# A hybrid encoder layer on one core: the first loads on two queues, the second input tile in halves

## The chip, the core and the metric

The kernel runs on one core of one Trainium2 chip. A core has a matrix engine (TensorE, in the profile PE, with its weight loads as PEld), a vector engine (VectorE, DVE), a scalar engine (ScalarE, ACT), GpSimd (POOL) and SyncE (SP). Each engine takes its instructions in order. A DMA is issued by an instruction on an engine's queue, SP's or ACT's here, and its bytes are moved by 16 DMA engines. A tile in the on-chip memory has 128 partitions. The metric is the time of one execution on the device in microseconds (us), the median of several runs.

## The reference, cut

The layer norms its input, projects it once into the columns of two attention mixers (a sliding window with grouped queries and sinks, and a neighbourhood attention on a grid of tokens), norms both results, projects them back, and ends with a gated MLP with a short convolution and a last norm. Sequence and width are both 1024.

```python
hn = rmsnorm(h, norm_mix[l])
proj = jnp.einsum('bsd,de->bse', hn, w_in[l])
qa, ka, va, qb, kb, vb = jnp.split(proj, splits, axis=-1)
...
o_a = window_gqa_sink(qa, ka, va, sink[l])
o_b = neighbourhood_attention(..., rpb[l])
mix = jnp.concatenate([rmsnorm(o_a, norm_a[l]), rmsnorm(o_b, norm_b[l])], axis=-1)
h = h + jnp.einsum('bse,ed->bsd', mix, w_out[l])
hn = rmsnorm(h, norm_ffn[l])
h = h + conv_gated_mlp(hn, w_gate[l], w_up[l], conv_w[l], conv_b[l], w_down[l])
return rmsnorm(h, norm_final)
```

The change lies at the start of the combined projection.

## The kernel before, in words

The input is held transposed, as eight tiles `xT[k]` of 128 features by 1024 tokens (k = 0 to 7, 512 KB each, 4 KB in a partition). The weights `w_in[m]` of one block of 128 output columns are 128 by 8 by 128; index j of the middle dimension belongs to input tile k = j.

Every product is made from two halves of precision: a float32 tile is split into a high part, rounded by ACT (a Copy into float32r), and a low part, the difference, made by DVE. So an input tile gives `xgh` and `xgl` (L125 and L126, and for the first tile L532 and L533), and a weight tile gives `whi` and `wlo` (L108 and L109, and for the first weights L537 and L538). One block of a product is three matmuls of 128x512: high by high (L113), the weights' high part by the input's low part (L114), the weights' low part by the input's high part (L115). The norm's gain is put in with the split, from a column of the parameters tile `par`; the factor 1/rms comes later, on the products.

The kernel starts with small memsets on GpSimd, a table load and a one-column activation (`warm`, L95) on ACT, and eight matmuls on `ones` (L98). Then the first two column blocks (`first`, m = 0 and 1) are projected together while the input arrives: for every input tile k, for each half h of the tokens, one block of three matmuls for m = 0 (into bank `pj`) and one for m = 1 (into bank `o`), so 12 matmuls for each tile (L566 to L571). For the squares that the norm needs, ACT squares each input tile (L139) and DVE adds them up (L141). The third block (m = 2, bank `s`) follows, then the sums for 1/rms (L150 to L161), and then the rest of the projections and the attention.

All loads of the head stand in SP's queue in this order: `par` (L82, 60 KB), the first half of input tile 0 (L522), the weights j = 0 of both blocks (L524, 64 KB each), the second half of tile 0 (L525), the weights j = 1 to 3 of both blocks (L527, 192 KB each), input tiles 1 to 3 whole (L515), the weights j = 4 to 7 of both blocks (L105), tiles 4 to 7 (L515), and then constants and further weights. The `raw` weights have two staging buffers and the high and low parts three each, so the loads of L105 wait until DVE has made the low parts of the first weights, and their split waits until PE has used the first weights; what stands behind such a load in SP's queue waits with it.

PE's instructions keep the order in which the code writes them (`manual_schedule`). The order of ACT, DVE, POOL and SP is made when the kernel is built, by a list scheduler that estimates when operands are ready and prefers what was written first.

Of the kernel before, what the change touches and what calls it, by code (L numbers as in the profile page):

```python
# [13 lines left out]
F32 = mybir.dt.float32  # L14
F32R = mybir.dt.float32r
AF = mybir.ActivationFunctionType
ALU = mybir.AluOpType
PSUM = bass.MemoryType.PSUM

D, S, HD = 1024, 1024, 64  # L20
KT = D // 128
NB = S // 128
HALF = 512
# [22 lines left out]
C_NMIX, C_NFFN, C_NFIN, C_NA, C_NB, C_CW, C_CB, C_SINK = 0, 8, 16, 24, 28, 32, 98, 120  # L46
# [5 lines left out]
def hybrid_layer(tc, xT, w_in, w_out, w_gate, w_up, w_down, small, sink, rpb, consts, rope, out):  # L52
    nc = tc.nc
    with ExitStack() as ctx:
# [6 lines left out]
        wpool = inner("weights", 3)  # L61
# [6 lines left out]
        def big(name, tag, dt=F32):  # L68
            return lpool.tile([128, S], dt, name=name, tag=tag, bufs=slots[tag])
# [7 lines left out]
        f32 = lambda ap: ap.bitcast(F32)  # L77
        tsl = lambda h: slice(h * HALF, (h + 1) * HALF)
        col = lambda c: par[:, c:c + 1]

        par = cpool.tile([128, C_END], F32, name="par")
        nc.sync.dma_start(par[:, 0:C_SINK], small)  # L82
        ones = cpool.tile([128, 128], F32, name="ones")
        nc.gpsimd.memset(ones, 1.0 / D)
        eps = cpool.tile([128, 1], F32, name="eps")
        nc.gpsimd.memset(eps, EPS)
        cst = cpool.tile([128, K_END], F32, name="cst")
        ident = cst[:, K_ID:K_ID + 128]


        ctx.enter_context(tc.manual_schedule(engines={mybir.EngineType.PE}))
# [20 lines left out]
        def block(ps, w, x, h, first, last):  # L112
            nc.tensor.matmul(ps, w[0], x[0][:, tsl(h)], start=first, stop=False)  # L113
            nc.tensor.matmul(ps, w[0], x[1][:, tsl(h)], start=False, stop=False)  # L114
            nc.tensor.matmul(ps, w[1], x[0][:, tsl(h)], start=False, stop=last)  # L115
# [7 lines left out]
        def split_scaled(src, scale, name, tag):  # L123
            hi, lo = big(name + "h", tag, F32R), big(name + "l", tag, F32R)
            nc.scalar.activation(hi, src, AF.Copy, scale=scale)  # L125
            nc.vector.scalar_tensor_tensor(lo, src, scale, f32(hi[:, :]), op0=ALU.mult, op1=ALU.subtract)  # L126
            return hi, lo
# [380 lines left out]


        xg, first = [None] * KT, [Project(0), Project(1)]  # L510
        xts, sqs = [], []

        def load_x(k):
            xt = big("xt", "op")
            nc.sync.dma_start(xt, xT[k])  # L515
            xts.append(xt)


        xt0 = big("xt", "op")
        xts.append(xt0)  # L520
        head = [[wpool.tile([128, 4, 128], dt, name="w0", tag=tag, bufs=n) for dt, tag, n in ((F32, "raw", 2), (F32R, "whi", 3), (F32R, "wlo", 3))] for _ in first]
        nc.sync.dma_start(xt0[:, 0:HALF], xT[0, :, 0:HALF])  # L522
        for p, (raw, _, _) in zip(first, head):
            nc.sync.dma_start(raw[:, 0:1], w_in[p.m, :, 0:1, :])  # L524
        nc.sync.dma_start(xt0[:, HALF:S], xT[0, :, HALF:S])  # L525
        for p, (raw, _, _) in zip(first, head):
            nc.sync.dma_start(raw[:, 1:4], w_in[p.m, :, 1:4, :])  # L527
        xg[0] = big("xgh", "xg", F32R), big("xgl", "xg", F32R)
        g0 = col(C_NMIX)

        def first_x(h):
            nc.scalar.activation(xg[0][0][:, tsl(h)], xt0[:, tsl(h)], AF.Copy, scale=g0)  # L532
            nc.vector.scalar_tensor_tensor(xg[0][1][:, tsl(h)], xt0[:, tsl(h)], g0, f32(xg[0][0][:, tsl(h)]), op0=ALU.mult, op1=ALU.subtract)  # L533

        def first_w(ks):
            for raw, hi, lo in head:
                nc.scalar.activation(hi[:, ks], raw[:, ks], AF.Copy)  # L537
                nc.vector.tensor_tensor(lo[:, ks], raw[:, ks], f32(hi[:, ks]), op=ALU.subtract)  # L538

        first_x(0)  # L540
        first_w(slice(0, 1))
        first_x(1)
        first_w(slice(1, 4))
        for p, (_, hi, lo) in zip(first, head):
            p.w = [(hi[:, j, :], lo[:, j, :]) for j in range(4)]
        for k in range(1, 4):
            load_x(k)
        for p in first:
            p.w += load_w(w_in[p.m, :, 4:8, :])
        for k in range(4, KT):  # L550
            load_x(k)
        nc.sync.dma_start(cst, consts)
        nc.sync.dma_start(par[:, C_SINK:C_END], sink.partition_broadcast(128))
        nsink = cpool.tile([128, 8], F32, name="nsink")
# [5 lines left out]
        for _ in range(2):  # L560
            t = quarters(big("f", "mix"))
# [2 lines left out]
        banks = [[bank("pj", "pj") for _ in range(2)], [bank("o", "o") for _ in range(2)]]  # L564
        acc = None
        for k in range(KT):  # L566
            if k:
                xg[k] = split_scaled(xts[k], col(C_NMIX + k), "xg", "xg")
            for h in range(2):
                for p, ps in zip(first, banks):  # L570
                    block(ps[h], p.w[k], xg[k], h, k == 0, k == KT - 1)  # L571
# [3 lines left out]
        raw, hi, lo = big("raw3", "mix"), big("whi3", "mix", F32R), big("wlo3", "mix", F32R)  # L575
# [84 lines left out]
        for g in range(2):  # L660
            for b in range(NB):
                q, t = unit_window(g, b)
# [49 lines left out]
        for u in range(len(flat)):  # L712
            q, t, need, kind = flat[u]
# [46 lines left out]
        for h in range(2):  # L760
            wide = widen(vb2[h], "pt")
            for i in range(4):
                x = mix[4 + i][:, tsl(h)]
                hi, lo = (t[:, tsl(h)] for t in mg[4 + i])
# [462 lines left out]
        for i, (p, j, c) in enumerate(order):  # L1227
            prepare(i + 6, i + 4)
            f, n = PARTS[c]
# [123 lines left out]
```

## Time and profile before

| What | Value |
|---|---|
| Median of 3 runs | 1135.11 us (1134.78 to 1135.58) |
| The profiled execution, its own time | 1135.27 us |
| Span that the profile covers | 1133.5 us |
| Mean granted TensorE clock | 0.983 |
| DMA traffic of the whole kernel | 147.03 MB, mean 130 GB/s |

The span is shorter than the execution's time by 1.8 us, which lie around the profiled instructions. A timeline row gives the start in us from the span's start, the length, the engine, the line of the kernel, the operation, the tile written and the tiles read, the shapes and a count; in brackets stands how long the engine had been idle before it, and what ended that idle time. In a view by stretches, a row gives for each engine the busy time in the stretch (and the number of instructions), then the clock granted to TensorE as a share of full speed, the mean busy share of the DMA engines and the GB/s that they moved. Starts of matmuls are taken from the trace; their ends are modelled, and matmuls overlap, so the distance between two starts is the pace.

### The profile page before, as it was taken

The numbers are of one execution on the slowest core, as the hardware profiler recorded it, in microseconds if no ns is written. First come the engines' busy times: TensorE is split into PE (matmuls) and PEld (weight loads), VectorE is DVE, ScalarE is ACT, GpSimd is POOL, SyncE is SP. The second block draws the span as 40 slices with busy tenths as digits, with TensorE's granted clock in tenths as the row PEclk, the third lists the DMA queues.
The fourth block names the chain that finished last, engine by engine and source line by source line (L and its number), as shares of the span: only waits on it lengthen the run. The fifth ranks groups of instructions, "written<-read, shape, count | busy, mean of one in ns | idle before, by whom it ended". The sixth has DMA issues, their size and how long they took to land.

```text
span 1133.5 us, 14918 instructions
## 1 busy us (share of the span) xinstructions
PE 1087.3 (96%) x5124; PEld 904.3 (80%) x5124; DVE 853.2 (75%) x1549; ACT 549.9 (49%) x1033; POOL 105.9 (9%) x186
## 2 busy tenths in 40 slices
PE   8969999999999989999899999999999899999995
PEld 6857888888878878888688888888888688888884
DVE  5556888766689667899988778877877868886843
ACT  6335777656667534444443344334343645543531
POOL 0302333232223100000000000000000000000001
PEclk8989999999999999999899999999999999999997
DMA  7252120333215217303432223222322698865723
GB/s 262 61 126 79 52 57 29 80 93 88 74 36 150 94 47 256 134 29 109 181 128 103 102 93 121 103 102 93 121 103 93 222 322 280 280 226 169 258 83 148
DMA packets 67708, 147.03 MB, mean 130 GB/s; under 512 B 8112, under 2 KB 16816, under 8 KB 67632
## 3 DMA queue, kind: packets, MB, share of 16 engines
q1 hardware_dynamic: 57552, 121.04, 33.4%
q10 hardware_dynamic: 10080, 25.04, 5.9%
q8 instruction: 40, 0.66, 0.2%
q14 instruction: 36, 0.29, 0.1%
HBM read 103.58 MB, written 28.57 MB: 117 GB/s over the span
## 4 chain that ended last, share of the span: by engine, by line
PE 87%; DVE 6%; DMA 2%; ACT 2%; issue 1%; SPq 0%; POOLq 0%; ACTq 0%; DVEq 0%
PE pj L113 7%; PE pj L114 7%; PE pj L115 7%; PE dn L797 6%; PE dn L799 6%; PE dn L798 6%; PE z L797 4%; PE z L798 4%; PE z L799 4%; PE s L273 3%; PE x L797 3%; PE x L798 3%; PE x L799 3%; PE y L799 3%; PE y L798 3%; PE y L797 3%
## 5 line engine op out<-in xcount | busy, mean ns | idle before, releaser
L786 ACT ACTIVATE whi<-ws 128x512 fp32r<-128x512 f32 (+1 forms) x100 | 60.1, 623 | 126.2 <-DVE ws L903 86.0
L797 PE MATMUL dn<-xd,whi 128*128 128x512 f32 x308 | 120.0, 390 | 0.0
L799 PE MATMUL dn<-xd,wlo 128*128 128x512 f32 x308 | 119.8, 389 | 0.0
L798 PE MATMUL dn<-xd,whi 128*128 128x512 f32 x308 | 119.8, 389 | 0.0
L797 PE MATMUL z<-hg,whi 128*128 128x512 f32 x264 | 103.2, 391 | 2.2 <-DVE gs L953 2.2
L113 PE MATMUL pj<-xgh,whi 128*128 128x512 f32 x248 | 103.7, 418 | 0.0
L799 PE MATMUL z<-hg,wlo 128*128 128x512 f32 x264 | 103.2, 391 | 0.2 <-DVE wlo L787 0.2
L798 PE MATMUL z<-hg,whi 128*128 128x512 f32 x264 | 103.0, 390 | 0.0
L299 ACT ACTIVATE p<-p,nm 128x385 f32<-128x385 f32 (+3 forms) x128 | 75.1, 587 | 55.5 <-DVE nm L295 51.5
L115 PE MATMUL pj<-xgh,wlo 128*128 128x512 f32 x248 | 97.8, 394 | 0.0
L114 PE MATMUL pj<-xgl,whi 128*128 128x512 f32 x248 | 97.5, 393 | 0.0
L303 POOL TENSOR_SCALAR p<-p,sm 128x384 f32<-128x384 f32 (+1 forms) x128 | 73.2, 584 | 237.1 <-DVE sm L301 217.9
L787 DVE TENSOR_TENSOR wlo<-raw,whi 128x512 fp32r<-128x512 f32 (+1 forms) x102 | 66.7, 672 | 24.2 <-ACT whi L786 24.2
L786 ACT ACTIVATE whi<-raw 128x512 fp32r<-128x512 f32 (+1 forms) x102 | 61.0, 612 | 45.3 <-DMA raw<-in_w_down_dram 11.0
L787 DVE TENSOR_TENSOR wlo<-ws,whi 128x512 fp32r<-128x512 f32 (+1 forms) x100 | 67.0, 683 | 20.6 <-ACT whi L786 20.4
L309 DVE TENSOR_TENSOR pl<-pt,ph 128x384 fp32r<-128x384 f32 (+2 forms) x108 | 63.2, 588 | 23.2 <-ACT ph L308 22.1
L308 ACT ACTIVATE ph<-pt 128x384 fp32r<-128x384 f32 (+2 forms) x108 | 55.2, 513 | 38.4 <-PE pt L408 30.9
L1209 POOL TENSOR_TENSOR y<-y,wide 128x512 f32<-128x512 f32 x4 | 5.1, 1280 | 734.1 <-ACT y L1208 734.1
L1110 ACT ACTIVATE xd<-xd 128x512 fp32r<-128x512 f32 x77 | 47.5, 627 | 53.5 <-DMA xd<-x 51.7
L797 PE MATMUL y<-hg,whi 128*128 128x512 f32 x176 | 69.3, 394 | 2.9 <-ACT whi L786 2.9
L799 PE MATMUL y<-hg,wlo 128*128 128x512 f32 x176 | 69.6, 395 | 2.2 <-DVE wlo L787 2.2
L797 PE MATMUL x<-hg,whi 128*128 128x512 f32 x176 | 68.8, 391 | 1.4 <-ACT c L937 1.4
(199 smaller groups left out, 2660.7 us busy)
## 6 DMA issues: line engine op xcount, KB each, us to landing
xd<-x SPq DMA_DIRECT2D x77, 256.0 KB, 4.9
raw<-in_w_down_dram SPq DMA_DIRECT2D x72, 256.0 KB, 3.5
raw<-in_w_gate_dram SPq DMA_DIRECT2D x22, 512.0 KB, 3.5
raw<-in_w_up_dram SPq DMA_DIRECT2D x22, 512.0 KB, 3.8
x<-c ACTq DMA_DIRECT2D x22, 512.0 KB, 2.8
raw<-in_w_in_dram SPq DMA_DIRECT2D x32, 256.0 KB, 3.2
raw<-in_w_down_dram SPq DMA_DIRECT2D x36, 192.0 KB, 3.8
x<-t ACTq DMA_DIRECT2D x11, 512.0 KB, 5.8
```

What stands on the lines that cost most here:

```text
L113: nc.tensor.matmul(ps, w[0], x[0][:, tsl(h)], start=first, stop=False)
L114: nc.tensor.matmul(ps, w[0], x[1][:, tsl(h)], start=False, stop=False)
L115: nc.tensor.matmul(ps, w[1], x[0][:, tsl(h)], start=False, stop=last)
L299: nc.scalar.activation(p[:, j, 0:e], p[:, j, 0:e], AF.Exp, bias=nm, scale=-1.0, accum_out=sm[:, j:j + 1])
L303: nc.gpsimd.tensor_scalar(p[:, i, 0:m], p[:, i, 0:m], sm[:, i:i + 1], 1.0, op0=ALU.mult, op1=ALU.mult)
L308: nc.scalar.activation(ph[:, 0:n], ps[:, 0:n], AF.Copy)
L309: nc.vector.tensor_tensor(pl[:, 0:n], ps[:, 0:n], f32(ph[:, 0:n]), op=ALU.subtract)
L786: nc.scalar.activation(hi, src, AF.Copy)
L787: nc.vector.tensor_tensor(lo, src, f32(hi[:, :, :]), op=ALU.subtract)
L797: nc.tensor.matmul(ps, w[0], x[0], start=first and i == 0, stop=False, skip_group_check=True)
L798: nc.tensor.matmul(ps, w[0], x[1], start=False, stop=False, skip_group_check=True)
L799: nc.tensor.matmul(ps, w[1], x[0], start=False, stop=last and i == len(ws) - 1, skip_group_check=True)
```

## The change

The parameters and the first weights are issued from ACT's queue, ahead of everything else on ACT in the code; SP's queue starts with the input. Input tile 1 is loaded in two halves, like tile 0, and split in two halves by the same code. The order of the splits in the code is: first half of tile 0, weights j = 0, second half of tile 0, weights j = 1 to 3, then the two halves of tile 1. Tiles 2 to 7 are loaded and split as before. The functions `load_x` and `split_x` take the place of the earlier `load_x` and `first_x`.

```diff
         par = cpool.tile([128, C_END], F32, name="par")
-        nc.sync.dma_start(par[:, 0:C_SINK], small)
+        nc.scalar.dma_start(par[:, 0:C_SINK], small)
...
+        def load_x(k, parts=1):
+            xt = big("xt", "op")
+            n = S // parts
+            for i in range(parts):
+                nc.sync.dma_start(xt[:, i * n:(i + 1) * n], xT[k, :, i * n:(i + 1) * n])
+            return xt
+
+        head = [[wpool.tile([128, 4, 128], dt, name="w0", tag=tag, bufs=n) for dt, tag, n in ((F32, "raw", 2), (F32R, "whi", 3), (F32R, "wlo", 3))] for _ in range(2)]
+        for ks in (slice(0, 1), slice(1, 4)):
+            for m, (raw, _, _) in enumerate(head):
+                nc.scalar.dma_start(raw[:, ks], w_in[m, :, ks, :])
+        xts = [load_x(0, 2), load_x(1, 2)]
...
         xg, first = [None] * KT, [Project(0), Project(1)]
-        nc.sync.dma_start(xt0[:, 0:HALF], xT[0, :, 0:HALF])
-        for p, (raw, _, _) in zip(first, head):
-            nc.sync.dma_start(raw[:, 0:1], w_in[p.m, :, 0:1, :])
-        nc.sync.dma_start(xt0[:, HALF:S], xT[0, :, HALF:S])
-        for p, (raw, _, _) in zip(first, head):
-            nc.sync.dma_start(raw[:, 1:4], w_in[p.m, :, 1:4, :])
...
+        def split_x(k, h):
+
+            g = col(C_NMIX + k)
+            hi, lo = (t[:, tsl(h)] for t in xg[k])
+            nc.scalar.activation(hi, xts[k][:, tsl(h)], AF.Copy, scale=g)
+            nc.vector.scalar_tensor_tensor(lo, xts[k][:, tsl(h)], g, f32(hi), op0=ALU.mult, op1=ALU.subtract)
...
-        first_x(0)
+        for k in range(2):
+            xg[k] = big("xgh", "xg", F32R), big("xgl", "xg", F32R)
+        split_x(0, 0)
         first_w(slice(0, 1))
-        first_x(1)
+        split_x(0, 1)
         first_w(slice(1, 4))
+        for h in range(2):
+            split_x(1, h)
...
-        for k in range(1, 4):
-            load_x(k)
+        for k in range(2, 4):
+            xts.append(load_x(k))
...
         for k in range(KT):
-            if k:
+            if k > 1:
                 xg[k] = split_scaled(xts[k], col(C_NMIX + k), "xg", "xg")
```

More of the change, by code (lines that the diff above doesn't have):

```diff
@@ L510, in hybrid_layer @@
         xg, first = [None] * KT, [Project(0), Project(1)]
[L511 to L522, printed above, removed]
-        for p, (raw, _, _) in zip(first, head):
-            nc.sync.dma_start(raw[:, 0:1], w_in[p.m, :, 0:1, :])
-        nc.sync.dma_start(xt0[:, HALF:S], xT[0, :, HALF:S])
-        for p, (raw, _, _) in zip(first, head):
[L527 to L533, printed above, removed]
+        def split_x(k, h):
[3 more added lines that the diff above has]
+            nc.vector.scalar_tensor_tensor(lo, xts[k][:, tsl(h)], g, f32(hi), op0=ALU.mult, op1=ALU.subtract)
         def first_w(ks):
@@ L550, in hybrid_layer @@
         for k in range(4, KT):
-            load_x(k)
+            xts.append(load_x(k))
         nc.sync.dma_start(cst, consts)
```

## The prediction

> **What bounds the kernel now.** I read the page first.
>
> ```profile
> span 1133.5 us, 14918 instructions
> PE 1087.3 (96%) x5124; PEld 904.3 (80%) x5124; DVE 853.2 (75%) x1549; ACT 549.9 (49%) x1033; POOL 105.9 (9%) x186
> PE 87%; DVE 6%; DMA 2%; ACT 2%; issue 1%; SPq 0%; POOLq 0%; ACTq 0%; DVEq 0%
> ```
>
> TensorE sets the time: busy 96% of the span, 87% of the chain that ended last. The change touches the first microseconds alone, so what it can win is what PE loses there, and then the shift has to reach the end. The timeline of PE shows the loss (start, length, line; k=0 is the first input tile, 12 matmuls, k=1 the second):
>
> ```profile
> 5.08 0.79 PE L113 MATMUL pj<-xgh,w 128*128 128x512 f32 x1 [0.31 <-ACT w L537]
> ...
> 8.98 0.39 PE L115 MATMUL o<-xgh,w 128*128 128x512 f32 x1
> 12.02 0.49 PE L113 MATMUL pj<-xgh,w 128*128 128x512 f32 x1 [2.66 <-ACT xgh L125]
> 13.34 0.79 PE L114 MATMUL pj<-xgl,w 128*128 128x512 f32 x1 [0.82 <-DVE xgl L126]
> ...
> 18.20 0.63 PE L113 MATMUL pj<-xgh,w 128*128 128x512 f32 x1
> ...
> 20.21 0.39 PE L113 MATMUL pj<-xgh,w 128*128 128x512 f32 x1
> ...
> 21.57 0.39 PE L113 MATMUL pj<-xgh,w 128*128 128x512 f32 x1
> ```
>
> k=0 ends at about 9.2, k=1 begins at 12.02 and is done at 18.20, k=2 at 21.57. At full pace (from 20.21 to 21.57 six matmuls start, 0.227 us apart, so 2.72 for a tile) k=2 would end at 9.2 + 2 x 2.72 = 14.6. So 6.9 us are lost: 2.8 waiting for the high part of tile 1, 0.8 for its low part, and the rest at half speed. Stretches of 3.41 us laid from 12.86 show that last part (length, PE busy, then PEclk, the granted clock):
>
> ```profile
> 9.45:12.86 3.41, 0.49 (x1) 0.19 (x1) 1.15 (x2) 2.04 (x3) 0.00 (x0) 0.98 0.99 386
> 12.86:16.27 3.41, 2.93 (x7) 2.35 (x8) 3.41 (x5) 3.41 (x5) 0.00 (x0) 0.50 0.95 319
> 16.27:19.69 3.42, 3.42 (x9) 2.64 (x9) 3.42 (x4) 3.42 (x5) 0.00 (x0) 0.52 1.02 413
> 419.05:422.46 3.41, 1.78 (x8) 1.13 (x6) 3.41 (x6) 1.89 (x3) 0.00 (x0) 1.00 0.00 0
> 555.58:558.99 3.41, 0.73 (x2) 0.30 (x2) 3.41 (x5) 0.63 (x1) 0.00 (x0) 0.98 0.62 245
> 24.00:26.00 2.00, 2.00 (x11) 1.65 (x10) 1.40 (x2) 2.00 (x3) 0.00 (x0) 1.00 0.04 6
> ```
>
> A stretch with 0.49 or 0.73 us of matmuls is followed by clock 0.50; one with 1.78 us is not; one full stretch (16.27 to 19.69) brings the clock back. The threshold lies between 0.73 and 1.78. [...]
>
> What is late is seen in the SP queue and on ACT (L515 issues whole tiles, L105 the weights of k=4 to 7, L527 those of k=1 to 3):
>
> ```profile
> 0.74 0.39 SPq L82 DMA_DIRECT2D par<-in_small_dram  x1
> 1.18 0.42 SPq L522 DMA_DIRECT2D xt<-in_xT_dram  x1
> 1.65 0.90 SPq L524 DMA_DIRECT2D w<-in_w_in_dram  x2
> 2.59 0.43 SPq L525 DMA_DIRECT2D xt<-in_xT_dram  x1
> 3.06 0.91 SPq L527 DMA_DIRECT2D w<-in_w_in_dram  x2
> 4.01 1.38 SPq L515 DMA_DIRECT2D xt<-in_xT_dram  x3
> 8.38 1.72 SPq L105 DMA_DIRECT2D raw<-in_w_in_dram  x2
> 10.15 1.84 SPq L515 DMA_DIRECT2D xt<-in_xT_dram  x4
> ```
>
> ```profile
> 0.73 1.28 ACT L95 ACT_TABLE_LOAD   x1 [0.73 <-PEq L1342]
> 2.02 0.20 ACT L95 ACTIVATE warm<-eps 128x1 f32<-128x1 f32 x1
> 4.11 0.72 ACT L532 ACTIVATE xgh<-xt,par 128x512 fp32r<-128x512 f32 x1 [1.88 <-DMA xt<-in_xT_dram]
> ...
> 6.38 0.72 ACT L532 ACTIVATE xgh<-xt,par 128x512 fp32r<-128x512 f32 x1 [0.80 <-DMA xt<-in_xT_dram]
> 7.19 0.52 ACT L537 ACTIVATE w<-w 128x384 fp32r<-128x384 f32 x1
> ...
> 8.63 0.53 ACT L537 ACTIVATE w<-w 128x384 fp32r<-128x384 f32 x1
> 10.82 1.15 ACT L125 ACTIVATE xgh<-xt,par 128x1024 fp32r<-128x1024 f32 x1 [1.67 <-DMA xt<-in_xT_dram]
> ...
> 12.82 1.14 ACT L125 ACTIVATE xgh<-xt,par 128x1024 fp32r<-128x1024 f32 x1
> ```
>
> Tile 1 is the eighth DMA, issued at 4.01 and landed at 10.8; ACT waited 1.67 us for it.
>
> **ACT's start.** Five DMAs go to ACT, the parameters first among them, issued at 0.74 as now: moving them costs nothing as long as the first half lands after them. On SP an issue costs 0.43 to 0.47 (0.74, 1.18, 1.65), so ACT is free at about 3.05; the table load (1.28) and the warm activation (0.20), which stood there unhidden but early, now follow: 4.5. The first split starts at 4.5 rather than 4.11. Bounds: 4.1 if the load stays ahead, 6.5 if issues from two engines slow each other to 0.86. I take 4.5, as the first half now lands by 3.7 (issued 0.44 earlier). PE starts at 5.5, 0.4 later. The second half is issued at 1.18, not 2.59, so its split no longer waits 0.80: it runs at 5.7, and k=0 ends at 8.8 (5.5, six matmuls with the low part's wait to 7.45, six times 0.227), 0.4 earlier than now.
>
> **Tile 1 and the weights.** By the shapes, parameters, two input tiles and the head weights are 60 + 1024 + 512 = 1596 KB in both kernels, and now all of it is issued by 3.05 rather than 4.4. Landing rates: from the second half (700 KB in order, 6.38) to the last head weight (1084 KB, 8.63) 171 KB/us with rows of 1.5 KB; from there to tile 1 (1596 KB, 10.82, rows of 4 KB) 234. The last weight's landing is its issue (3.5) plus the median of this row:
>
> ```profile
> w<-in_w_in_dram SPq DMA_DIRECT2D x2, 192.0 KB, 5.1
> ```
>
> The new pieces have rows of 1.5 and 2 KB, so both rates are bounds: from 316 KB at 3.7 the last piece lands at 9.1 (234) or 11.2 (171). I take 10.1. Which piece is last is not seen: weights on ACT's queue lose their place ahead of tile 1 and may land later than now (8.63), tile 1 earlier. The split of tile 1 in halves costs ACT 2 x 0.72 against 1.15 and DVE 2 x 0.75 against 1.28, but the first half frees PE after 0.72, and its low part comes 0.75 rather than 1.28 later:
>
> ```profile
> 7.14 0.75 DVE L533 SCALAR_TENSOR_TENSOR xgl<-xt,par,xgh 128x512 fp32r<-128x512 f32 x1 [1.12 <-ACT xgh L532]
> ...
> 12.00 1.28 DVE L126 SCALAR_TENSOR_TENSOR xgl<-xt,par,xgh 128x1024 fp32r<-128x1024 f32 x1 [2.26 <-ACT xgh L125]
> ...
> 14.34 1.28 DVE L126 SCALAR_TENSOR_TENSOR xgl<-xt,par,xgh 128x1024 fp32r<-128x1024 f32 x1
> ...
> 17.27 1.28 DVE L126 SCALAR_TENSOR_TENSOR xgl<-xt,par,xgh 128x1024 fp32r<-128x1024 f32 x1
> ```
>
> ACT works in order. If the first half's split goes before the last weight, k=1 starts at about 9.8; if behind it, at 10.1 + 0.53 + 0.72 = 11.35. Between: first matmul at 10.9, second (low part) at 11.65. The stretch to 12.86 then holds 0.5 + 1.2 = 1.7 us of matmuls, inside the unknown band but next to the 1.78 that kept the clock. So I let the clock stay, and k=1 ends at 11.65 + 11 x 0.227 = 14.15 instead of 18.20.
>
> **What is late next.** Tile 2. Its split is at 12.82 now, without a wait, so it lands by then, and its low part runs at 14.34 behind other DVE work. Its bytes end at 2108 KB; at 234 from 10.1 it lands at 12.3. High part by 13.7, low part by 14.9 (bounds 14.0 and 15.6, the present end). k=2 then ends at 14.9 + 11 x 0.227 = 17.4 instead of 21.57: 4.2 us won, bounds 3.5 and 5. DVE is next: the third tile's low part ends at 18.55 now, 0.7 earlier with tile 2's, and PE wants it at 17.6: 0.2 lost. The second half weights need the slots and staging buffers of the first: L105 waits for DVE on the last head weight (8.38 now; about 11.2 for the second of them), and x4 to x7, constants and all that SP holds wait behind it, 1.6 us later than 10.15. x1 to x3 and the backlog cover most of that; I take 0.6 for it and for the weight split at k=4, bounds 0 and 1.6. Sum: 4.2 - 0.2 - 0.6 = 3.4 us.
>
> **Does it reach the end?** From 24 to 26 the DMA share is 0.04: nothing is still under way from the head. ACT's stop before the late head work is a wait for PE and moves with it:
>
> ```profile
> ACT whi L108 <- PE pj L114: 3.1, 1, 3.1
> ```
>
> So everything behind shifts with PE. The orders of ACT, DVE and SP are made by the scheduler when the kernel is built and can change further on; I price that at 0, bounds -1 and +1. The profiled execution took 1135.27 (span 1133.5 and 1.8 around it), 0.16 above the median: 1135.1 - 3.4 = 1131.7.
>
> **Rivals.**
> The bytes decide (0.30). The last piece lands at 11.2 and ACT's order has tile 1 behind the weights: first matmul 12.45, low part 13.2. The stretch to 12.86 holds 0.4 us, the clock halves as now, and full stretches bring it back at 19.69 as now. Won: 13.34 - 13.2, up to 1.1 us if the piece lands at 10.3: 1134.0 to 1135.0, 1134.6. For it: the DMA share is 0.99 from 9.45 on. Against it: the earlier issue. [...]
>
> Slower (0.13). Weights and input interleave so that the last weight lands behind part of tile 2, and PE's unbroken run starts after 16.27 instead of 13.34. Then the stretch 16.27 to 19.69 is not full, and the clock returns one stretch later, at 23.10. By 23.10 PE now does, from 13.34, 6.35 / 0.44 + 3.41 / 0.227 = 29.4 matmuls (0.44: eleven steps from 13.34 to 18.20); then it would do 6.8 / 0.44 = 15.5. 14 x 0.227 = 3.2 us lost: 1138.3. It decides from a weight landing at about 14. Against it: 2108 KB at the slower rate from 3.7 land at 14.2 only if all of tile 2 goes first.
>
> Better (0.07): tile 2 lands by 11 and k=1 starts at 9: 5.5 to 6.4 won, 1129.2.
>
> **How the numbers follow.** The forecast has 0.50, own range 1130.3 to 1133.2. 8 in 10: from 1130.0 to 1136.0, leaving out the slower rival and the best of the better one. 0.2% (2.3 us) is about what a measurement of this kernel can tell from no change. Faster: forecast nearly whole and the better case, 0.54; same: the bytes' case and edges of both neighbours, 0.32; slower: 0.14.
>
> **What would show it.** The first ACTIVATE behind five ACTq issues at 4.5; k=1's first matmul at 10 to 11.4; clock 1.00 from 12.86 on; PE waiting next for tile 2's parts at about 14; k=2 done by 17.4. Clock 0.50 after 12.86 shows the bytes' case; a clock back only at 23 the slower one. The forecast is wrong if the shift at 30 us is not found again at the end.

## The result and the profile after

| What | Before | After |
|---|---|---|
| Median of 22 runs each | 1135.95 us (1134.44 to 1140.12) | 1133.90 us (1129.88 to 1138.39) |
| Ratio of the times, 95% interval | | 0.998 (0.9971 to 0.9989) |
| The profiled execution, its own time | 1135.27 us | 1133.22 us |
| Span that the profile covers | 1133.5 us | 1131.4 us |

The kernel became about 2 us faster; by the interval 1.2 to 3.3 us. The page of the kernel after (the span, the busy time of PE, the chain of work that ended last):

```profile
span 1131.4 us, 14922 instructions
...
PE 1086.2 (96%) x5124; PEld 902.6 (80%) x5124; DVE 852.1 (75%) x1550; ACT 549.2 (49%) x1034; POOL 109.8 (10%) x186
...
PE 86%; DVE 6%; DMA 4%; ACT 2%; issue 1%; POOLq 0%; SPq 0%; ACTq 0%; DVEq 0%
```

What bounds the kernel is the same; new in the chain is that the DMA's share rose from 2% to 4%. In the helpers that come up here the lines of after are 14 higher (L113 to L115 became L127 to L129, L108 and L109 became L122 and L123, L125 became L139). ACT's timeline of after:

```profile
0.73 0.41 ACTq L82 DMA_DIRECT2D par<-in_small_dram  x1
1.17 1.90 ACTq L101 DMA_DIRECT2D w<-in_w_in_dram  x4
3.10 1.28 ACT L109 ACT_TABLE_LOAD   x1 [3.10 <-issue]
...
4.50 0.71 ACT L530 ACTIVATE xgh<-xt,par 128x512 fp32r<-128x512 f32 x1
...
6.51 0.31 ACT L535 ACTIVATE w<-w 128x128 fp32r<-128x128 f32 x1 [1.10 <-DMA w<-in_w_in_dram]
...
8.17 1.32 ACT L530 ACTIVATE xgh<-xt,par 128x512 fp32r<-128x512 f32 x2
10.12 1.15 ACT L139 ACTIVATE xgh<-xt,par 128x1024 fp32r<-128x1024 f32 x1 [0.63 <-DMA xt<-in_xT_dram]
...
17.88 1.13 ACT L139 ACTIVATE xgh<-xt,par 128x1024 fp32r<-128x1024 f32 x1
18.92 0.61 ACT L122 ACTIVATE whi<-raw 128x512 fp32r<-128x512 f32 x1
```

Five issues, the table load, and the first split at 4.50. Both halves of tile 1 are split from 8.17 on without a wait (before: the whole tile at 10.82, after 1.67 us of waiting), and tile 2 at 10.12 (before 12.82). One thing is later: the second block's weights j = 0 make ACT wait 1.10 and are split at 6.51. The same split in before, and then SP's queue in after:

```profile
5.27 0.31 ACT L537 ACTIVATE w<-w 128x128 fp32r<-128x128 f32 x1 [0.24 <-DMA w<-in_w_in_dram]
```

```profile
0.74 1.33 SPq L95 DMA_DIRECT2D xt<-in_xT_dram  x3
...
4.07 1.75 SPq L95 DMA_DIRECT2D xt<-in_xT_dram  x4
```

SP issues three pieces of the input (both halves of tile 0, the first half of tile 1) by 2.07 and then none for 2 us; the second half of tile 1 goes out at 4.07. The view of SP's waits in the first 8 us of after says what it waited for (us in total, times, the longest):

```profile
SPq L95 <- DMA par<-in_small_dram: 2.0, 1, 2.0
```

SP waits for the parameters, which are the first load on ACT's queue and land 3.3 us after their issue, at 4.05. The half that is held back does not read them, and no run shows why its issue waits for them. With the halves alone, a kernel told of below in which SP issues all of the first loads, both halves of tile 1 are issued from 4.01 to 4.92 without a pause.

PE's timeline of after, and its stretches with the granted clock behind the busy times:

```profile
5.46 0.50 PE L127 MATMUL pj<-xgh,w 128*128 128x512 f32 x1 [0.85 <-ACT w L535]
...
9.54 0.40 PE L127 MATMUL pj<-xgh,w 128*128 128x512 f32 x1
...
12.52 0.39 PE L127 MATMUL pj<-xgh,w 128*128 128x512 f32 x1
...
15.26 0.39 PE L127 MATMUL pj<-xgh,w 128*128 128x512 f32 x1
...
17.98 0.39 PE L127 MATMUL pj<-xgh,whi 128*128 128x512 f32 x1
...
19.58 0.50 PE L127 MATMUL o<-xgh,whi 128*128 128x512 f32 x1 [0.76 <-ACT whi L122]
...
20.50 0.50 PE L129 MATMUL o<-xgh,wlo 128*128 128x512 f32 x1 [0.19 <-DVE wlo L123]
```

```profile
9.45:12.86 3.41, 3.41 (x16) 2.43 (x15) 2.32 (x3) 2.78 (x4) 0.00 (x0) 1.00 1.03 405
12.86:16.27 3.41, 3.41 (x17) 2.81 (x16) 2.97 (x3) 3.31 (x5) 0.00 (x0) 1.00 1.03 416
```

k=1 begins at 9.54 (before 12.02), k=2 at 12.52 (before 18.20) and k=3 at 15.26 (before 21.57), at full clock and without a wait. The first wait is in k=4, for the second block's weights j = 4 to 7.

The order of the 5124 matmuls is the same in both kernels, so the n-th one can be laid beside the n-th one of before. The **lead** below is how much earlier a matmul starts than the same matmul in the trace of before; each column stands at the time of that matmul there. The kernels of the rows are told further on.

| Lead in us at (us in before) | 12.0 | 22 | 30 | 360 | 380 | 406 | 440 | 600 | 950 | last matmul |
|---|---|---|---|---|---|---|---|---|---|---|
| before, second trace | 0.18 | 0.54 | 0.54 | 0.72 | 0.68 | 0.68 | -0.91 | 0.48 | -1.23 | -0.76 |
| after | 2.48 | 6.31 | 4.77 | 4.96 | 3.88 | 3.88 | 2.28 | 1.73 | 1.79 | 1.98 |
| after, second trace | 1.63 | 5.73 | 4.72 | 2.93 | 2.93 | 2.93 | 2.90 | 3.12 | 3.05 | 3.12 |
| halves alone | 1.95 | 4.79 | 4.15 | 4.61 | 4.22 | 4.21 | 2.66 | 4.19 | 2.20 | 2.67 |
| two queues alone | 0.76 | 4.84 | 4.84 | 5.23 | 4.58 | 4.58 | 2.95 | 4.54 | 2.46 | 2.93 |
| both and spare tile | 1.71 | 5.71 | 5.71 | 6.80 | 6.80 | 6.80 | 6.82 | 6.58 | 4.13 | 4.60 |
| the same, second trace | 2.31 | 6.18 | 6.18 | 4.81 | 4.84 | 4.84 | 4.85 | 6.71 | 4.75 | 5.20 |
| halves and spare tile | 1.75 | 4.59 | 4.17 | 3.00 | 1.95 | 1.95 | 0.34 | 2.39 | 0.08 | 0.30 |

So the head won 6.3 us, not the 2 that are left at the end: 1.5 are lost by 30 us, 1.1 between 360 and 380, 1.6 between 406 and 440. The first of these losses is in the two traces of after alike; the other two are not.

### The profile page after: what moved, and what is told of

It is laid out like the page before. It is cut to its first block, busy times and chain, and to the rows that moved or that the text cites. A ratio compares the mean times of both kernels' runs of the same rounds, so it can differ in the third digit from the quotient of the medians.

```text
span 1131.4 us, 14922 instructions
## 1 busy us (share of the span) xinstructions
PE 1086.2 (96%) x5124; PEld 902.6 (80%) x5124; DVE 852.1 (75%) x1550; ACT 549.2 (49%) x1034; POOL 109.8 (10%) x186
## 4 chain that ended last, share of the span: by engine, by line
PE 86%; DVE 6%; DMA 4%; ACT 2%; issue 1%; POOLq 0%; SPq 0%; ACTq 0%; DVEq 0%
PE pj L127 7%; PE pj L128 7%; PE pj L129 7%; PE dn L799 6%; PE dn L800 6%; PE dn L801 6%; PE z L799 4%; PE z L801 4%; PE z L800 4%; PE s L287 3%; PE x L799 3%; PE x L801 3%; PE x L800 3%; PE y L801 3%; PE y L799 3%; PE y L800 3%
## 5 line engine op out<-in xcount | busy, mean ns | idle before, releaser
L127 PE MATMUL pj<-xgh,whi 128*128 128x512 f32 x248 | 103.6, 418 | 0.0
L129 PE MATMUL pj<-xgh,wlo 128*128 128x512 f32 x248 | 97.8, 394 | 0.0
```

## The experiments

**Each half of the change alone.** In the first kernel (halves alone) all first loads stay on SP in the old order, and tile 1 is loaded and split in halves; in the second (two queues alone) tile 1 stays whole. Both diffs are against after.

```diff
-        nc.scalar.dma_start(par[:, 0:C_SINK], small)
+        nc.sync.dma_start(par[:, 0:C_SINK], small)
...
-                nc.scalar.dma_start(raw[:, ks], w_in[m, :, ks, :])
-        xts = [load_x(0, 2), load_x(1, 2)]
+        xts = [big("xt", "op") for _ in range(2)]
+        for k, h, ks in ((0, 0, slice(0, 1)), (0, 1, slice(1, 4)), (1, 0, None), (1, 1, None)):
+            nc.sync.dma_start(xts[k][:, h * HALF:(h + 1) * HALF], xT[k, :, h * HALF:(h + 1) * HALF])
+            if ks:
+                for m, (raw, _, _) in enumerate(head):
+                    nc.sync.dma_start(raw[:, ks], w_in[m, :, ks, :])
```

```diff
-        xts = [load_x(0, 2), load_x(1, 2)]
+        xts = [load_x(0, 2), load_x(1)]
...
-        for h in range(2):
-            split_x(1, h)
...
-            if k > 1:
+            if k:
```

> All first loads stay in SP's queue in the old order (parameters, first half of tile 0, weights j=0, second half, weights j=1 to 3, tile 1), but tile 1 is still loaded and split in halves. Theory Q (the two queues do it: bytes are issued sooner and the DMA engines stay full): tile 1's first half lands at 9.5 or later, PE begins k=1 at 10.5 to 11.5 instead of 9.5, and of the 6.3 us that PE has won at the end of k=1 to k=3 at most 4.5 are left; if the clock is halved around 13, at most 1.5. Theory H (the halves do it): PE begins k=1 by 10, the clock stays at 1.00, and 5.5 us or more are won by 18 us.

> Two queues as in the changed kernel, but tile 1 is loaded and split whole. Theory Q: tile 1 lands by 8.5, its high part is ready at about 9.6, its low part at about 10.9; PE waits some 0.9 us more in k=1 than the changed kernel, the clock stays at 1.00, and the start of the third block's matmuls (bank s) is within 0.6 us of the changed kernel's 30.4 us, because the weights of k=4 are waited for anyway. Theory H: k=1 begins at 10.8 or later and the clock is halved around 13; 3 us or more of the gain are gone.

Halves alone: 1133.06 us (10 runs), ratio 0.9976 (0.9958 to 0.9994). Two queues alone: 1134.69 (10 runs), ratio 0.9991 (0.9974 to 1.0009). PE's timeline of the kernel with the halves alone, then of the one with two queues alone:

```profile
10.07 0.50 PE L129 MATMUL pj<-xgh,w 128*128 128x512 f32 x1 [0.88 <-ACT xgh L532]
10.86 0.50 PE L130 MATMUL pj<-xgl,w 128*128 128x512 f32 x1 [0.29 <-DVE xgl L533]
```

```profile
7.54 0.79 PE L127 MATMUL o<-xgh,w 128*128 128x512 f32 x1 [0.75 <-ACT w L535]
...
11.26 0.40 PE L127 MATMUL pj<-xgh,w 128*128 128x512 f32 x1
```

What the DMA engines moved (last column GB/s, the share before it) in two stretches, in before, in halves alone, in two queues alone, and in after:

```profile
2.00:5.00 3.00, 2.77 (x13) 2.48 (x12) 0.14 (x1) 1.11 (x4) 0.00 (x0) 1.00 0.71 206
5.00:9.00 4.00, 3.63 (x12) 2.29 (x12) 2.24 (x5) 2.87 (x6) 0.00 (x0) 1.00 0.86 261
```

```profile
2.00:5.00 3.00, 2.72 (x13) 2.48 (x12) 0.18 (x1) 1.16 (x5) 0.00 (x0) 1.00 0.74 237
5.00:9.00 4.00, 3.59 (x12) 2.12 (x12) 2.21 (x6) 2.86 (x5) 0.00 (x0) 1.00 0.89 239
```

```profile
2.00:5.00 3.00, 2.51 (x14) 2.32 (x12) 0.00 (x0) 1.88 (x3) 0.00 (x0) 1.00 0.95 317
5.00:9.00 4.00, 2.70 (x7) 1.74 (x8) 2.11 (x5) 2.25 (x7) 0.00 (x0) 0.81 0.98 347
```

```profile
2.00:5.00 3.00, 2.61 (x14) 2.42 (x12) 0.00 (x0) 1.89 (x3) 0.00 (x0) 1.00 0.91 300
5.00:9.00 4.00, 3.14 (x10) 1.87 (x11) 2.77 (x6) 2.90 (x8) 0.00 (x0) 1.00 0.99 332
```

From 2 to 9 us one queue moves about 1.66 MB with and without the halves (3 x 206 + 4 x 261, 3 x 237 + 4 x 239), two queues 2.23 (after). With one queue the DMA engines are busy 0.71 to 0.74 of the time from 2 to 5 us, with two 0.91 to 0.95, and the second queue puts the stream ahead by 0.57 MB, 1.4 us at the 404 GB/s that before moves from 9 to 12 us. The halves win without any of that: the first matmul of k=1 needs 256 KB and a split of 0.7 us, not 512 KB and 1.15, and PE's hole of 2.66 us shrinks to 0.88, with the granted clock at 1.00 from 2 to 9 us and on to 12. So either part alone brings 4 to 5 us at 30 us, and they don't add up: both avoid the same stretch at half speed after 12.86. The two queues alone pay for their rate with a hole of 0.75 us, since the second block's first weights land late, and the granted clock of 0.81 between 5 and 9 us.

Neither theory of the two expectations came out whole. With the halves alone k=1 began at 10.07 and the clock stayed at 1.00, as theory H had it, but 4.8 us were won at 22 us and not 5.5. With the two queues alone k=1 began at 11.26; the third block began at 30.33, within 0.1 us of the changed kernel, as theory Q had it, but the clock did fall, earlier than either theory had it. In the measured time the halves alone are as good as the whole change, while the interval of the two queues alone (0.9974 to 1.0009) leaves open whether they changed anything.

**The same kernels a second time.** To see which losses belong to the code, after and before were traced again with no edit.

> The changed kernel once more, for its trace. Theory P (the clock's windows of 3.41 us run freely, so the loss of 1.6 us that the changed kernel's trace shows at 420 us depends on where a window falls in the 3.2 us hole there): the first 30 us repeat within 0.4 us, the times at which the granted clock changes, taken modulo 3.41 us, differ from the first trace's, and the loss at 420 us is there only if some window holds less than some 1 us of matmuls. Rival O (the changed order of instructions costs it): the loss of 1.6 us at 420 us and the wait of 1 us at 365 us come again at the same matmuls.

> The kernel before once more, for its trace. Theory P: the wait for tile 1 comes again (k=1 begins at 12.0 within 0.4), but the clock may stay at 1.00 after it, or fall at another time, and the hole of 3.2 us before 424 us may cost the clock this time. Rival O: the clock falls at the same matmuls as in the first trace, and not at 424 us.

After took 1132.13 us (one run, span 1130.3), before 1135.94 (span 1134.1). The head came again, if not quite: before starts k=1 0.18 us earlier than in its first trace, and after leads by 4.72 us at 30 us, but by 0.85 and 0.58 us less than in its first trace at 12 and 22 us, more than the 0.4 that was expected. The places of the later losses moved. Stretches of before in its first and in its second trace, then of after in its first and in its second (the eighth number, ahead of the DMA share, is the granted clock):

```profile
424.00:428.00 4.00, 3.96 (x17) 3.28 (x18) 1.88 (x3) 0.00 (x0) 0.00 (x0) 1.00 0.00 0
```

```profile
424.00:428.00 4.00, 4.00 (x13) 3.08 (x12) 0.78 (x2) 0.00 (x0) 0.00 (x0) 0.59 0.00 0
```

```profile
40.00:44.00 4.00, 3.97 (x22) 3.40 (x23) 2.44 (x4) 0.60 (x1) 0.00 (x0) 1.00 0.21 64
...
420.00:424.00 4.00, 3.85 (x10) 3.09 (x11) 1.29 (x3) 0.00 (x0) 0.00 (x0) 0.59 0.00 0
```

```profile
40.00:44.00 4.00, 3.92 (x14) 3.44 (x15) 2.49 (x5) 0.60 (x1) 0.00 (x0) 0.57 0.23 63
...
420.00:424.00 4.00, 2.87 (x12) 2.36 (x13) 2.27 (x4) 0.53 (x1) 0.00 (x0) 1.00 0.00 0
```

PE has a hole of 3.2 us near 420 us in all four traces, where it waits for DVE. One execution of the same code loses the clock behind it and another doesn't, for before as for after. In the first trace of before the clock is halved from 12.86 to 19.69, twice 3.41 us, and from 408.67 to 412.08, once 3.41 us; such a length is called a window here. Where the windows begin differs between traces of the same code: in the second trace of before the clock falls at 424.76, 16.09 us or 4.7 windows after the 408.67 of the first, and with after one trace has a fall at 420.74 and the other at 40.47, about 111.4 windows apart. Half speed for one window costs about 1.6 us in the table of leads, about half of its 3.41 us. The loss near 40 us is not behind a hole: PE runs narrow matmuls there (the last section has them). So of the 3 us that after loses in its first trace behind 30 us, the 1.6 at 420 us are not the change's: before loses them too, in its second trace.

The 1.1 us between 360 and 380 us are another kind of loss. The transfer of `kb` on SP's queue in before, in after, and in the second trace of after, and the matmul in after that waits for it:

```profile
363.57 0.46 SPq L214 DMA_DIRECT2D kb<-ka  x1
```

```profile
358.89 0.46 SPq L228 DMA_DIRECT2D kb<-ka  x1
...
365.51 0.39 PE L287 MATMUL s<-kb,q 128*128 128x256 f32 x1 [0.80 <-DMA kb<-ka]
```

```profile
361.10 0.46 SPq L228 DMA_DIRECT2D kb<-ka  x1
```

In after the transfer is issued 4.68 us earlier than in before, about the lead, and lands 6.6 us later, just after PE wants it; in the second trace of after, with a lead of 2.93 there, PE doesn't wait. In before PE doesn't wait either. PE waits for `kb` again with two queues alone (0.37) and in the kernel with one queue and the spare tile (0.80), and in no trace of before or of the spare tile with two queues. The wait is shown; that a transfer with so little slack happens to take longer in some executions is only read from these traces, and why was not tried.

**The wait at k=4.** The high and low parts have three slots each. The second block's parts of the weights j = 4 to 7 need one again that PE frees when it is done with the first block's old weights; in ACT's built order their split then stands behind the split of a later input tile (17.88, then 18.92, with no idle time between). This kernel gives them a tile that lies unused there.

```diff
-        def load_w(src, n=4):
+        def load_w(src, n=4, spare=None):
...
+            if spare is None:
...
+            else:
+                both = spare[:, :].rearrange("p (s j c) -> p s j c", s=2, c=128)
+                hi, lo = both[:, 0], both[:, 1]
...
-            p.w += load_w(w_in[p.m, :, 4:8, :])
+            p.w += load_w(w_in[p.m, :, 4:8, :], spare=big("w48", "mix", F32R) if p.m else None)
```

> The changed kernel; the high and low parts of the second block's weights j=4 to 7 go to a free tile of their own instead of a slot that the first block's first weights hold, so their split no longer waits for PE. Theory K (the 1.3 us that PE loses at k=4 come from that slot and its place on ACT): the wait for whi at k=4 (0.76 in the changed kernel's trace) and for wlo (0.19) go, PE's third block (bank s) begins 1.0 to 1.4 us earlier than in the changed kernel, that is 29.0 to 29.4 us in a run whose clock stays full in the head. Rival: the weights land late, and the same wait stands with a DMA behind it.

> The two-queue kernel with the spare tile a second time, the same code. Theory (a window of the clock gate falls on the holes near 40, 420 and 895 us by chance of its phase): the lead at 30 to 365 us is 5.5 to 6.5 us again, while the losses of about 1.6 us stand at other places than in its first trace (there only at 895 us) or at more or fewer of the three. Rival (the kernel itself sets where they fall): the same one loss at 895 us and none at 420 us. Median 1130.4 to 1131.8 by both.

The two sets of runs gave 1131.02 us (4 runs), ratio 0.9954 (0.9941 to 0.9967), and 1131.13 (6 runs), ratio 0.9959 (0.9943 to 0.9975). ACT's and PE's timelines of its first trace:

```profile
13.97 0.63 ACT L126 ACTIVATE whi<-raw 128x512 fp32r<-128x512 f32 x1
14.62 0.63 ACT L126 ACTIVATE w<-raw 128x512 fp32r<-128x512 f32 x1
```

```profile
18.58 0.39 PE L131 MATMUL pj<-xgh,whi 128*128 128x512 f32 x1
...
19.26 0.39 PE L131 MATMUL o<-xgh,w 128*128 128x512 f32 x1
```

Both weight tiles are split in a row, four us earlier than the second was, PE passes k=4 without a wait, and the lead at 30 us is the lead at 22 us (5.71 and 6.18; after lost 1.54 and 1.01 there). The wait for the slot is thus shown as the cause of the loss by 30 us; how much of it was ACT's order behind the slot was not tried apart. In the measured time the spare tile brings 2.4 to 3.0 us against after (by the ratios 0.9954 and 0.9959 against 0.998; the second one's interval still overlaps that of after), more than the 1.0 to 1.5 us of the head. The places of the later losses differ between its two traces, as the theory of chance has it: in the first trace the lead falls only at 895 us (by 2.4, from 6.58 to 4.13), in the second at 40 us as well (from 6.18 to 4.60) and behind 415 us (from 6.42 to 4.85).

**The spare tile with one queue.** The same edit on the kernel with the halves alone, against which the diff is.

```diff
-            p.w += load_w(w_in[p.m, :, 4:8, :])
+            p.w += load_w(w_in[p.m, :, 4:8, :], spare=big("w48", "mix", F32R) if p.m else None)
```

> One queue as before, tile 1 in halves, and the spare tile for the second block's weights j = 4 to 7. Theory (the two queues bring 1 us or less at the end once the wait at k = 4 is gone): k=1's first matmul at about 10.1 as with one queue before, no wait for weights at k = 4, PE ahead of the kernel before by 4.5 to 5.2 us at 30 us, and a median 0 to 1 us above the two-queue kernel with the spare tile. Rival (the second queue also serves what comes later, such as the loads behind the weights of j = 4 to 7): the lead at 30 us is under 4.3 and the median is 1.5 us or more above it.

1134.75 us (12 runs), ratio 0.9986 (0.9973 to 1.0000), beside 1131.13 for two queues with the spare tile on the same chip. My theory fell in its sizes: the lead at 30 us is 4.17, and the median stands 3.6 us higher, the numbers of the rival. There was little to mend on one queue: the halves alone wait 0.34 us at k=4 (the lead falls 0.64 by 30 us), since PE comes there later, and the spare tile brings nothing there (0.9976 without it, 0.9986 with it). Taken together, by the medians the second queue is worth nothing with the wait at k=4 (after 0.998, halves alone 0.9976) and 3.6 us without it. The head shows 1.5 to 2.0 us of that (5.71 and 6.18 against 4.17); where the rest comes from no run shows. That the second queue serves later loads, the rival's mechanism, is not shown either: this one trace lost 1.2 us near 40 us, 1.05 to the wait for `kb`, 1.6 from 406 to 440 and 2.3 between 600 and 950 us.

**Holding the clock.** If the later holes cost the clock by chance, matmuls of 128x128 on `ones` in four of them should stop that, in after, in before, and with the spare tile.

```diff
+        def busy(n, tag):
+            ps = psum.tile([128, HALF], F32, name="busy", tag=tag)
+            for _ in range(n):
+                nc.tensor.matmul(ps[:, 0:128], ones, ones, start=True, stop=True)
...
+            if n == 6:
+                busy(5, "pt")
```

> The changed kernel with matmuls on the constant tile of ones, whose results nobody reads, in four holes of PE behind the head (some 8.5 us at 66, 3.2 at 417, 3.1 and 2.2 at 552, 2.2 at 894). Theory P (holes cost the clock when a window of 3.41 us falls on them): the granted clock stays at 1.00 in all four, only the fall at 404 (narrow matmuls) and the one behind the last product are left; 4 to 7 us less than the changed kernel's 1133.9, so 1127 to 1130. Rival O (the holes cost only their own length): no gain, or a loss of up to 1 us where the added matmuls end late.

> The kernel before with the same matmuls in the same four holes. Theory P: it gains as well, 3 to 6 us against the kernel before, and the changed kernel with them (e6_after_warm) is faster than this one by the whole head gain of 4.0 to 5.5 us, more than the 2.05 us between the two kernels without them. Rival O: the two differ by 2 us as the kernels do without the added matmuls, so the rest of the head's gain is lost somewhere else.

> Both additions to the changed kernel: the free tile for the second block's late weights and the matmuls in the four holes. Theories P and K together: 1.0 to 1.4 us less than e6_after_warm, 1126 to 1129, faster than both kernels. Rival: the head's 1.3 us is taken back by the wait for the next weights, and the time is that of e6_after_warm.

After with them: 1132.95 (6 runs), ratio 0.9965 (0.9951 to 0.9978). Before with them: 1135.51 (11 runs), 0.9993 (0.9985 to 1.0002). With the spare tile: 1129.83 (6 runs), 0.9948 (0.9932 to 0.9964), whose interval holds both ratios of the spare tile alone. This was a miss as a test, for the clock fell nevertheless in most places. Stretches of after with them, at the hole near 895 us:

```profile
891.66:895.07 3.41, 0.61 (x7) 0.42 (x5) 3.41 (x6) 1.57 (x3) 0.00 (x0) 1.00 0.06 23
895.08:898.49 3.41, 3.41 (x8) 2.73 (x9) 1.73 (x3) 0.00 (x0) 0.00 (x0) 0.50 0.58 183
```

Too few were put in there: 0.61 us of PE work in a window of 3.41 was followed by half speed. Near 555 us they were enough: before with them and the spare tile with them keep the clock there, which all traces without them lose for 3.4 or 6.8 us. After and before with them differ by 2.56 us, the rival's number; since the clock fell in both, the test says neither that the clock hides part of the change's gain nor that it doesn't. The fastest version found is the change with the spare tile, with or without these matmuls; between the two nothing can be told.

## Why the prediction was right or wrong

**The time** came out inside the range of 1130.0 to 1136.0, 2.2 us above the forecast and 0.7 above the forecast's own range (1130.3 to 1133.2). Of the 2.2 us, 0.8 are the median of before, 1135.11 over 3 runs and 1135.95 over 22; the gain was 2.05 us by the medians where 3.4 was forecast. That it came so near is in part luck: a gain in the head that was too small in the sum and a loss behind it that was priced at nothing met halfway.

**ACT's start** was right: five issues, the table load, and the first split at 4.50 (predicted 4.5), PE at 5.46 (5.5). k=0 ended at 9.5, not 8.8: I had both blocks' first weights there in time, and the second block's landed late, so that ACT split the second half of tile 0 at 6.73 and not at 5.7. From 2 to 5 us SP's queue moved 0.71 MB and ACT's 0.19; that the input's pieces held the weights up is read from this and was not tested. That moving the parameters costs nothing failed too: SP waited 2.0 us for them.

**Tile 1, tile 2 and the bytes.** The clock stayed at 1.00, as forecast and against the rival in which the bytes decide. But the rates that I took as bounds, 171 and 234 KB/us, counted only the pieces up to the one that had landed, while tiles behind it were already moving: before moves 1.66 MB from 2 to 9 us, where the count had 1084 KB at 8.63. With two queues 300 and 332 GB/s were moved; ACT split the halves of tile 1 from 8.17 on without a wait between them, where the last piece of the head was to land at 10.1 (bounds 9.1 to 11.2), and tile 2, for which it waited, from 10.12 (predicted 12.3). That came about although the issues ended later than I had them: not by 3.05, but at 4.50, for SP's wait. So PE waited for neither, k=1 began at 9.54 rather than 10.9, and 6.3 us were won at 22 us rather than 4.2: the case called better (0.07). The share of the DMA engines between 2 and 5 us rose from 0.71 to 0.91, and what they moved from 206 to 300 GB/s.

**The queue and the weights at k=4.** The mechanism (slots and ACT's place for the split) was right and stood in the sum; its size was 1.0 to 1.5 us where 0.6 was taken (bounds 0 and 1.6). The DVE term of 0.2 isn't seen: no wait stands between 9.54 and 19.58.

**"Does it reach the end?"** is the step that failed. It was priced at 0, bounds 1 either way, on the ground that nothing is under way at 24 us and everything shifts with PE. Up to 360 us that is what the trace shows (4.77, 4.96). Behind it a transfer with no slack took 1.1 us in this trace, and the clock was lost near 40 or 420 us in one execution and not in the next, 1.6 to 1.8 us each time. The test that the prediction named, the shift at 30 us found again at the end, failed: 4.77 became 1.98, and 3.12 in the second trace. A single trace of before can't price this, since its own second trace ends 0.76 us behind the first.

**What stays open.** The leads of 4.2 to 4.8 us at 30 us stand beside 2.3 us in the measured time (1.2 to 3.3). Two traces of each kernel show losses by chance in both, so they should cancel in the medians; that they fall on after more often than on before, or that the wait for `kb` does, is possible, and two traces don't decide it. Over all kernels, the loss near 40 us is in four of nine traces with a changed head and in none of three with the old one, and the wait for `kb` in three of nine and none of three; that points the same way and is too little to decide it.

## What to carry to other kernels

When loads at the start are issued one behind the other, read the DMA share and the GB/s before taking a landing rate from them: here a share of 0.71 left room that a second queue filled (0.91 to 0.95), and counting landings in order missed what was already moving behind them. When loads are moved to a second queue, look at what the first one then waits for (here 2.0 us for the parameters). The gain in the head lasted only up to the next resource that was timed for the old pace (6.31 us at 22 us, 4.77 at 30); look for the next slot and for the order of the engine that frees it, and remove that wait in the same change. And when a gain of 2 us is sought in a kernel with holes of 2 to 3 us in TensorE's work, trace the same code twice before explaining where the gain went.

## What the runs showed of the hardware

How little work keeps the clock is known better for matmuls of 512 columns. Stretches of the second trace of before, and of the first one with the spare tile:

```profile
421.34:424.75 3.41, 1.38 (x6) 1.16 (x7) 3.18 (x6) 0.81 (x2) 0.00 (x0) 1.00 0.00 0
424.76:428.17 3.41, 3.41 (x10) 2.62 (x9) 0.43 (x1) 0.00 (x0) 0.00 (x0) 0.50 0.00 0
```

```profile
412.34:415.75 3.41, 1.67 (x8) 1.05 (x6) 3.41 (x6) 1.79 (x3) 0.00 (x0) 1.00 0.00 0
415.75:419.16 3.41, 1.92 (x8) 1.61 (x9) 2.64 (x5) 0.63 (x1) 0.00 (x0) 1.00 0.00 0
```

A window of 3.41 us with 1.38 us of matmuls was followed by half speed, one with 1.67 was not. The prediction had the threshold between 0.73 and 1.78. The edge isn't sharp in these busy times: with two queues alone a window with 1.52 us (550.23 to 553.65) was followed by half speed, and in after one with 1.48 (550.45 to 553.86) was not. The windows of the second kernel are laid by the time of its other clock changes, so its 1.67 is as good as that placing.

Busy time alone doesn't decide it, which the prediction's threshold took for granted. In after PE is busy through the whole window up to 403.68, nearly all of it with matmuls of one column (`ss` from `ones`, 128x1, the sums for 1/rms), and the clock is halved behind it:

```profile
400.26:403.68 3.42, 3.42 (x32) 3.38 (x32) 1.18 (x2) 1.94 (x3) 0.00 (x0) 1.00 0.30 120
403.68:407.09 3.41, 3.41 (x11) 2.73 (x11) 0.84 (x3) 0.26 (x1) 0.00 (x0) 0.50 0.48 153
```

The same holds of before (405.26 to 408.67, 3.41 us busy). The window ahead of the loss near 40 us in the second trace of after (37.06 to 40.47) has 2.30 us of PE work, more than the 1.67 that kept the clock, in matmuls of 1 and of 128 columns. That narrow matmuls count for less is read from these windows; no run varied the width alone.

One small early load came later with two queues. The second block's first 64 KB of weights are the third issue of ACT's queue in after (the second of four that begin at 1.17 and take 1.90, so at about 1.65) and the fourth of SP's in before (the second of two that begin at 1.65, so at about 2.1); ACT split them at 6.51 in after and at 5.27 in before, waiting for them in both. Over the seven traces with two queues the split is at 5.94 to 7.17, always behind a wait.

SP's pause from 2.07 to 4.07 in after was not expected. In before SP issued ten DMAs one behind the other up to 5.39. The wait for the parameters, 1.8 to 2.0 us, is in all seven traces with two queues and in none with one. Another load in the parameters' place, or their issue from SP, was not tried, so what the pause costs is not known.
